# Other steps in the timetable of layer 0's mixers: a case on one core of Trainium2

## The chip, the cores and the metric

The kernel runs on one core of one Trainium2 chip. The metric is the device time of one execution in microseconds (us). Before the change three runs gave a median of 2450.46 us (2445.37 to 2455.84). The engines are named by their short names in the rows: PE is TensorE (PEld its weight loads), DVE VectorE, ACT ScalarE, POOL GpSimd and SP SyncE.

## The reference

A two-layer encoder works on 2048 tokens of 1024 channels. Layer 0 splits its projection into a head group with HGRN2 (the "a" side) and one with RWKV7 (the "b" side); layer 1 is a gated linear recurrence (RG-LRU). Each layer modulates its input by a conditioning vector and ends in a projection, a gated residual and a layer norm.

```python
cond = jax.nn.silu(c)
for l in range(DEPTH):
    mod = cond @ ada_w[l] + ada_b[l]
    shift, scale, gate = jnp.split(mod, 3, axis=-1)
    h = x * (1.0 + scale[:, None]) + shift[:, None]
    if l % 2 == 0:
        u = h @ ev_w_in[e]
        qA, fA, iA, gA, rB, kB, vB, zB, gB = jnp.split(u, EVEN_SPLITS, axis=-1)
        oA = hgrn2_chunkwise(qA, fA, iA, lbs[e], a_norm_g[e])
        oB, vf = rwkv7_mix(rB, kB, vB, zB, ...)
        mixed = jnp.concatenate([oA * silu(gA), oB * silu(gB)], axis=-1)
        y = mixed @ ev_w_out[e]
    else:
        ...
    x = layer_norm(DEEPNORM_ALPHA * x + (1.0 + gate[:, None]) * y, ln_g[l], ln_b[l])
```

HGRN2 works in chunks of 64 tokens: a decay log_f, its running sum b, products of queries and keys under exp(b_t - b_s), and a state carried from chunk to chunk. RWKV7 is a recurrence with a rank-one correction per token:

```python
sa = jnp.einsum('bhvk,bhk->bhv', S, a_t)
S = S * w_t[:, :, None, :] + sa[..., None] * b_t[:, :, None, :] + v_t[..., None] * k_t[:, :, None, :]
y_t = jnp.einsum('bhvk,bhk->bhv', S, r_t)
```

The kernel does it in chunks of 64 tokens too, which asks for the inverse of a triangular matrix per chunk. It is solved in pieces of 16 tokens, these are merged to 32, and these to 64.

## The kernel before, in words

The sequence is worked in two super-blocks (`sb`, 1024 tokens), each in two blocks (`b`, 512 tokens). For each super-block layer 0 runs a mixer stage, `mix0`, and an output projection; then layer 1 does the same. In the trace the mixers of layer 0 lie at 35 to 780 us and at 880 to 1604 us.

A float32 product of large matrices is made of three products of split operands (`mm3`, L431 to L433). One projection of 128 channels for 512 tokens (`pp_...`) is 24 matmuls.

The order of TensorE's work in `mix0` is written out by a timetable. The generator `projections()` goes in steps of six projection matmuls: 16 steps for the low-rank inputs of RWKV, 192 for the projections, and then the gates. Beside it stands a list of tasks, each a generator with the step at which it is due. After each step every due task runs to its next `yield n`, and is due again n steps later. There are four groups of heads (g0 to g3) with two blocks each (b0, b1); a block is named g1b0 and the like. For each there are three tasks: `rate_steps` (decay rates, matmuls `pw`), `b_steps` (RWKV) and `a_steps` (HGRN2). A fourth kind, `late_modulation_steps`, computes modulation columns that are wanted later: eight weight tiles are loaded and accumulated on VectorE (`acc`, L166, L168), then the columns are summed over the partitions by a matmul (`pm`, L190).

Only TensorE is put in the order of the timetable (`tc.manual_schedule(engines={nc.tensor.engine})`). The other engines' order is decided by the scheduler, which sees the program in the order in which the generators emitted it.

The steps of `b_steps`, by their products on TensorE, counted from the block's start: `pss` (L831) at 2, the chunk products `psc` (L872) at 8 and 10, a solve of 16 x 16 pieces on VectorE and GpSimd, the 32-token merge with `plq` (L961) at 22, `pzq` (L971) at 24 and `plx` (L990) at 26, the 64-token merge `pz` (L1001) at 28, then `pwv`, `pmq`, the states `pn` (one chunk per step), `py` at 42 and `pvr` at 44. Between `pzq` and `plx` lie four copies to `x_b` on ScalarE (L975) and a transpose to `xm` on VectorE (L977). Before `pss` is used, a logarithm is taken on ScalarE (L362), which loads another activation table before and the usual one after (L356, L351).

The steps of `a_steps`: a preparation with exponentials and a logarithm on ScalarE (L606 to L608), the decay (L610), its scan (L612), two more rows and an exponential (L614 to L617), then per level two halves of a decay tile `w_a` (L631, L632), its exponential (L633) and a product with the query (L634), used by the scores `sc_a` (L646); four steps after the preparation come `pv_a` and the scores of levels 5 and 0, then the others, the state `pst` (L717, L729), the output `po_a` and a norm.

Of the kernel before, what the change touches and what calls it, by code (L numbers as in the profile page):

```python
# [68 lines left out]
def tile_encoder(  # L69
# [21 lines left out]
    NSB = NT // SBT  # L91
# [57 lines left out]
    def V(name, i):  # L149
        o = VOFF[name] + i  # L150
        return vec[:, o : o + 1]
# [27 lines left out]
    def mod_cols(l, j, acc, wtile):  # L179

        for k in range(KT):
            w = wtile(j, k)
            nc.sync.dma_start(w, ada_w[l, k * P : (k + 1) * P, j * BLK : (j + 1) * BLK])
            mod_add(acc, w, k, first=k == 0)

    def mod_vec(l, j, acc):

        pm = ps.tile([P, 4], F32, name=f"pm{l}_{j}", tag="ta")
        for i in range(4):
            nc.tensor.matmul(pm[:, i : i + 1], acc[:, i * P : (i + 1) * P], ones, start=True, stop=True)  # L190
        mod_bias(l, j, pm)

    def mod_gate(l, n, acc):

        pg = ps.tile([P, BLK], F32, name=f"pg{l}_{n}", tag="ta")
        nc.tensor.matmul(pg[0:1], ones, acc, start=True, stop=True)
        gr = up.tile([P, BLK + 3], F32, name=f"gr{l}_{n}", tag="u")[0:1, 0:BLK]
        nc.sync.dma_start(gr, ada_bg[l][:, n * BLK : (n + 1) * BLK])
        nc.vector.scalar_tensor_tensor(out=gr, in0=pg[0:1], scalar=1.0, in1=gr, op0=ALU.add, op1=ALU.add)
        nc.sync.dma_start(gate_dr[l][:, n * BLK : (n + 1) * BLK], gr)  # L200
# [51 lines left out]
    for j in (1, 3):  # L252
        mod_vec(0, j, accs[j])

    def late_modulation_steps(l, js):

        wt = ("a_e", "a_lf", "a_w", "a_w")
        for i, j in enumerate(js):
            acc = tp.tile([P, BLK], F32, name=f"acc{l}_{j}", tag=("a_b", "a_kz")[i % 2])

            def wtile(j, k):
                t = wt[k % 4]
                return tp.tile([P, BLK], F32, name=f"adw{l}_{j}_{k}", tag=t, bufs=2 if t == "a_w" else 1)

            mod_cols(l, j, acc, wtile)
            yield 6
            if j < 4:
                mod_vec(l, j, acc)
            else:
                mod_gate(l, j - 4, acc)  # L270
# [78 lines left out]
    def ln_exp_after(ins):  # L349
        with tc.issue_after(ins.ins), tc.high_priority():  # L350
            nc.scalar.preload_act_table_set(LN_EXP)  # L351
# [245 lines left out]
    def a_steps(hh, sb, b, us):  # L597
# [17 lines left out]
        kf = t2k("a_e")  # L615
        nc.scalar.activation(kf, kz, AF.Exp)
        nc.vector.tensor_sub(kz, kz, bb)  # L617

        st = st_tiles[0]
        v128 = lambda t: t.rearrange("p (j two t) -> p j two t", two=2, t=64)  # L620
# [55 lines left out]
        for j in range(4):  # L676
            js = slice(j * P, (j + 1) * P)
# [37 lines left out]
        for j in range(4):  # L715
            js = slice(j * P, (j + 1) * P)
# [20 lines left out]
        for j in range(4):  # L737
            js = slice(j * P, (j + 1) * P)
# [31 lines left out]
    xd = cst.tile([P, 8, 32], F32, name="xd")  # L770
    nc.gpsimd.memset(xd, 0.0)

    def rate_steps(p, sb, b, lr, sgi_of):

        sgi = sgi_of[p, b] = tp.tile([P, 2, BLK], F32, name=f"sgi_{p}_{sb}_{b}", tag="sgi")
        w2a2_sb = tp.tile([P, P], F32, name=f"w2a2_{p}_{sb}_{b}", tag="w2a2")
        nc.sync.dma_start(w2a2_sb, w2a2[:, p * P : (p + 1) * P])
        yield 2
        ls = slice(b * BLK, (b + 1) * BLK)

        pws = [ps.tile([P, BLK], F32, name=f"pw_{p}_{sb}_{i}_{b}", tag="tb", bufs=2) for i in range(2)]
        for i in range(2):
            rows = slice(64 * i, 64 * i + 64)
            nc.tensor.matmul(pws[i], w2a2_sb[rows], lr[rows, ls], start=True, stop=True)
        for i, bias in enumerate(("w0", "a0")):
            last = nc.scalar.activation(sgi[:, i], pws[i], AF.Sigmoid, bias=V(bias, p))
        ln_exp_after(last)
# [23 lines left out]
    def b_steps(p, sb, b, us, sgi_of):  # L811
# [168 lines left out]
        for hb in range(4):  # L980
            rs_ = slice(32 * hb, 32 * hb + 32)
            o_ = 32 * (hb % 2)
            nc.gpsimd.tensor_copy(tt[rs_, :, o_ : o_ + 32], x32[rs_])
        yield 2
        plx = ps.tile([P, 8, 32], F32, name=f"plx_{nm}", tag="tb", bufs=2)
        for c in range(8):
            for hd in range(2):
# [180 lines left out]
    def low_rank(sb, hs, lr, w_first):  # L1168
        l2 = [None, None]

        def evac_shift(b, pt):
            l2[b] = up.tile([P, BLK + 3], F32, name=f"l2_{sb}_{b}", tag="u")[:, 0 : BLK + 1]
            nc.scalar.copy(l2[b][:, 1 : BLK + 1], pt)
            if "lora" not in carry:
                nc.gpsimd.memset(l2[b][:, 0:1], 0.0)
            else:
                nc.gpsimd.tensor_copy(l2[b][:, 0:1], carry["lora"])
            lc = sp_.tile([P, 1], F32, name=f"lc_{sb}_{b}", tag="lc", bufs=2)
            nc.gpsimd.tensor_copy(lc, l2[b][:, BLK : BLK + 1])
            carry["lora"] = lc  # L1180

        def evac(b, pt):
            lrb = lr[:, b * BLK : (b + 1) * BLK]
            nc.vector.tensor_sub(lrb, pt, l2[b][:, 1 : BLK + 1])
            nc.vector.tensor_add(lrb, lrb, l2[b][:, 0:BLK])
            nc.scalar.activation(lrb[0:64], lrb[0:64], AF.Tanh)

        if sb == 0:
            yield from proj_start_steps(((f"z{sb}_1", w_first[0], evac_shift), (f"z{sb}_0", w_first[1], evac)), hs)
        else:  # L1190
            yield from proj_steps(wf_dr[1], f"z{sb}_1", hs, evac_shift, w_first[0])
            yield from proj_steps(wf_dr[0], f"z{sb}_0", hs, evac)

    def mix0(sb, hs, w_first):


        lr = tp.tile([P, SBT], F32, name=f"lr{sb}", tag="lr")
        sgi_of, tail = {}, []
        ub = [[[None, None] for _ in range(3)] for _ in range(4)]
        ua = [[[None, None] for _ in range(3)] for _ in range(4)]  # L1200

        def projections():
            yield from low_rank(sb, hs, lr, w_first)
            for g in range(4):
                for i in range(3):
                    key = f"b{sb}_{i}_{g}"
                    yield from proj_steps(w_ev[16 + 4 * i + g], key, hs, evac_lerp(key, i, g, ub[g][i]))
                for i in (1, 2, 0):
                    ct = 4 * i + g
                    key = f"a{sb}_{ct}"  # L1210
                    yield from proj_steps(w_ev[ct], key, hs, evac_u(key, (0, ct), 0, ua[g][i]))
            yield from gate_steps(
                0, sb, hs, w_ev, lambda k: 12 + k if k < 4 else 28 + k, (0, 1, 2, 4, 5, 6, 3, 7), tail,
                [dict(tag="lr"), dict(tag="sgi")],
            )

        tasks = []
        if sb == 0:
            tasks.append((18, late_modulation_steps(0, (4, 5))))
        if sb == NSB - 1:  # L1220
            tasks.append((18 if NSB > 1 else 36, late_modulation_steps(1, range(6))))
        for g in range(4):
            for b in range(2):
                early = 4 if g == 3 and b else 0
                tasks.append((34 + 48 * g + 24 * b - early, rate_steps(g, sb, b, lr, sgi_of)))
                tasks.append((40 + 48 * g + 24 * b - early, (g, b, b_steps, ub)))
                tasks.append((64 + 48 * g + 24 * b, (g, b, a_steps, ua)))

        tasks = [[at, task] for at, task in tasks]
        steps = projections()  # L1230
        now = 0
        with tc.manual_schedule(engines={nc.tensor.engine}):
            while tasks or steps is not None:
                if steps is not None and next(steps, "end") == "end":
                    steps = None
                now += 1
                for entry in list(tasks):
                    if entry[0] > now:
                        continue
                    if isinstance(entry[1], tuple):  # L1240
                        g, b, make, us = entry[1]
                        entry[1] = make(g, sb, b, us[g], sgi_of) if make is b_steps else make(g, sb, b, us[g])
                    wait = next(entry[1], None)
                    if wait is None:
                        tasks.remove(entry)
                    else:
                        entry[0] = now + wait
        return tail, load_wo(0, sb, w_evo, [
            tp.tile([P, n, BLK], F32, name=f"wo0_{sb}_{i}", tag=tag, bufs=bufs)
            for i, (n, tag, bufs) in enumerate(WO0)  # L1250
        ])
# [114 lines left out]
```

## Time and profile before

| | us |
|---|---|
| median of 3 runs | 2450.46 |
| profiled execution | 2446.24 |
| its span, first to last instruction | 2444.5 |
| TensorE busy | 2208.4 |
| VectorE busy | 1454.8 |
| ScalarE busy | 1256.6 |

One execution is recorded by the hardware profiler. A row of the timeline gives the start in the span, the duration, the engine, the line of the kernel, and in brackets the idle time of the engine before the instruction with what ended it. Matmuls of one kind that follow each other are one row with their count. [...]

### The profile page before, as it was taken

To read this page: it belongs to the slowest core of one execution; us is meant where nothing else is said; L and a number is where in the kernel's file an instruction comes from. 1 tells how busy PE (TensorE), PEld (TensorE's weight loads), DVE (VectorE), ACT (ScalarE), POOL (GpSimd) and SP (SyncE) were. 2 spreads that over 40 slices of the span, in tenths; PEclk is the share of its full clock that TensorE was granted. 3 is DMA by queue.
4 is the path that set the end of the run, shared out by engine and by line. 5 is a ranking of instruction groups with operands and counts; after the bars stand their busy time and mean duration, and the time that the engine had idled before them with its cause. 6 is when DMAs were issued, how large, how long until landed. Compare 5 with 4: busy or idle time off the path is not lost. (4 is left out here: it accounts for less than half of the span.)

```text
span 2444.5 us, 45532 instructions
## 1 busy us (share of the span) xinstructions
PE 2208.4 (90%) x18400; PEld 1738.7 (71%) x18400; DVE 1454.8 (60%) x2697; ACT 1256.6 (51%) x2027; POOL 557.2 (23%) x586
## 2 busy tenths in 40 slices
PE   5989989999987998899999999989986999996998
PEld 4767767677766876677776777768765778774776
DVE  6546667566644677565666755356766156766166
ACT  4344556545566433454455556654666344666332
POOL 3311112111112222111111111122433232433231
PEclk7989999999998999999999999989998999998999
DMA  7310111111424645111111123254313544113542
GB/s 289 93 37 24 41 32 41 38 38 38 118 70 128 207 152 175 34 34 43 25 42 35 37 83 97 72 204 143 104 65 120 169 141 137 67 57 122 167 137 103
DMA packets 185938, 229.82 MB, mean 94 GB/s; under 512 B 65912, under 2 KB 99320, under 8 KB 185728
## 3 DMA queue, kind: packets, MB, share of 16 engines
q1 hardware_dynamic: 185728, 226.92, 29.1%
q8 instruction: 144, 2.36, 0.4%
q14 instruction: 66, 0.54, 0.1%
HBM read 175.46 MB, written 51.39 MB: 93 GB/s over the span
## 5 line engine op out<-in xcount | busy, mean ns | idle before, releaser
L431 PE MATMUL pp_g<-hl_h,wh_g 128*128 128x512 f32 x512 | 212.3, 415 | 40.8 <-ACT go L574 40.8
L433 PE MATMUL pp_g<-hh_h,wl_g 128*128 128x512 f32 x512 | 204.6, 400 | 2.0 <-POOL wl_g L368 2.0
L431 PE MATMUL po<-hl_wo,wh_mx 128*128 128x512 f32 x448 | 179.3, 400 | 28.9 <-DVE hl_wo L368 24.1
L432 PE MATMUL pp_g<-hh_h,wh_g 128*128 128x512 f32 x512 | 204.9, 400 | 0.0
L433 PE MATMUL po<-hh_wo,wl_mx 128*128 128x512 f32 x448 | 177.4, 396 | 0.0
L432 PE MATMUL po<-hh_wo,wh_mx 128*128 128x512 f32 x448 | 177.2, 396 | 0.0
L368 POOL TENSOR_TENSOR wl_g<-raw_g,wh_g 128x512 fp32r<-128x512 f32 x64 | 87.2, 1363 | 377.5 <-ACT wh_g L367 342.7
L431 PE MATMUL pp_b<-hl_h,wh_b 128*128 128x512 f32 x384 | 168.5, 439 | 5.0 <-ACT cr_b L805 5.0
L431 PE MATMUL pp_a<-hl_h,wh_a 128*128 128x512 f32 x384 | 168.7, 439 | 0.0
L432 PE MATMUL pp_b<-hh_h,wh_b 128*128 128x512 f32 x384 | 153.7, 400 | 0.0
L433 PE MATMUL pp_a<-hh_h,wl_a 128*128 128x512 f32 x384 | 153.5, 400 | 0.0
L432 PE MATMUL pp_a<-hh_h,wh_a 128*128 128x512 f32 x384 | 153.3, 399 | 0.0
L433 PE MATMUL pp_b<-hh_h,wl_b 128*128 128x512 f32 x384 | 153.0, 398 | 0.0
L431 PEld LDWEIGHTS pp_g<-hl_h,wh_g 128*128 128x128 f32 x512 | 99.5, 194 | 64.7 <-ACT go L574 41.7
L368 POOL TENSOR_TENSOR wl_a<-raw_a,wh_a 128x512 fp32r<-128x512 f32 x48 | 67.7, 1416 | 329.1 <-ACT wh_a L367 329.1
L568 DVE TENSOR_TENSOR go<-go,oi 128x512 f32<-128x512 f32 x64 | 46.8, 733 | 160.6 <-ACT go L564 144.9
L368 POOL TENSOR_TENSOR wl_mx<-raw_mx,wh_mx 128x512 fp32r<-128x512 f32 x64 | 80.7, 1265 | 269.1 <-ACT wh_mx L367 269.1
L368 POOL TENSOR_TENSOR wl_b<-raw_b,wh_b 128x512 fp32r<-128x512 f32 x48 | 66.5, 1391 | 271.1 <-ACT wh_b L367 270.1
L431 PEld LDWEIGHTS po<-hl_wo,wh_mx 128*128 128x128 f32 x448 | 86.0, 192 | 48.4 <-DVE hl_wo L368 24.9
L433 PEld LDWEIGHTS pp_g<-hh_h,wl_g 128*128 128x128 f32 x512 | 99.2, 194 | 25.2 <-POOL wl_g L368 3.5
L432 PEld LDWEIGHTS pp_g<-hh_h,wh_g 128*128 128x128 f32 x512 | 99.4, 194 | 19.2
L433 PE MATMUL pp_c<-hh_h,wl_c 128*128 128x512 f32 x256 | 102.2, 400 | 8.6 <-POOL wl_c L368 8.6
(355 smaller groups left out, 5707.4 us busy)
## 6 DMA issues: line engine op xcount, KB each, us to landing
adw<-in_ada_w_dram SPq DMA_DIRECT2D x96, 256.0 KB
oi<-o_dr SPq DMA_DIRECT2D x64, 256.0 KB
m_dr<-go SPq DMA_DIRECT2D x56, 256.0 KB
raw_b<-in_w_ev_dram SPq DMA_DIRECT2D x48, 256.0 KB
raw_a<-in_w_ev_dram SPq DMA_DIRECT2D x48, 256.0 KB
raw_g<-in_w_ev_dram SPq DMA_DIRECT2D x32, 256.0 KB
wo<-in_w_evo_dram SPq DMA_DIRECT2D x32, 256.0 KB
raw_mx<-m_dr SPq DMA_DIRECT2D x32, 256.0 KB
```

Of the source, the lines that this page charges most:

```text
L368: return (eng or nc.vector).tensor_tensor(out=lo, in0=src, in1=hi.bitcast(F32), op=ALU.subtract)
L431: nc.tensor.matmul(pt, ah, bl, start=first, stop=False)
L432: nc.tensor.matmul(pt, ah, bh, start=False, stop=False)
L433: nc.tensor.matmul(pt, al, bh, start=False, stop=last)
L568: nc.vector.tensor_mul(go[b], go[b], oi[b])
```

## The change

It changes numbers in the timetable and adds one `yield`:

```diff
-    def late_modulation_steps(l, js):
+    def late_modulation_steps(l, js, gap):
...
             mod_cols(l, j, acc, wtile)
-            yield 6
+            yield gap
...
         kf = t2k("a_e")
         nc.scalar.activation(kf, kz, AF.Exp)
         nc.vector.tensor_sub(kz, kz, bb)
+        yield 2
...
-    def rate_steps(p, sb, b, lr, sgi_of):
+    def rate_steps(p, sb, b, lr, sgi_of, ahead):
...
-        yield 2
+        yield ahead
...
             nc.gpsimd.tensor_copy(tt[rs_, :, o_ : o_ + 32], x32[rs_])
-        yield 2
+        yield 4
         plx = ps.tile([P, 8, 32], F32, name=f"plx_{nm}", tag="tb", bufs=2)
...
         if sb == 0:
-            tasks.append((18, late_modulation_steps(0, (4, 5))))
+            tasks.append((10, late_modulation_steps(0, (4, 5), 14)))
         if sb == NSB - 1:
-            tasks.append((18 if NSB > 1 else 36, late_modulation_steps(1, range(6))))
+            tasks.append((4 if NSB > 1 else 38, late_modulation_steps(1, range(6), 9 if NSB > 1 else 4)))
         for g in range(4):
             for b in range(2):
-                early = 4 if g == 3 and b else 0
-                tasks.append((34 + 48 * g + 24 * b - early, rate_steps(g, sb, b, lr, sgi_of)))
-                tasks.append((40 + 48 * g + 24 * b - early, (g, b, b_steps, ub)))
-                tasks.append((64 + 48 * g + 24 * b, (g, b, a_steps, ua)))
+                at = 48 * g + 24 * b - (2 if g == 3 and b else 0)
+                tasks.append((34 + at if g or b else 2, rate_steps(g, sb, b, lr, sgi_of, 2 if g or b else 32)))
+                tasks.append((40 + at if g or b else 42, (g, b, b_steps, ub)))
+                tasks.append((62 + 48 * g + 24 * b, (g, b, a_steps, ua)))
```

In steps: in every RWKV block `plx` and all that follows it come two steps later. The HGRN2 task starts two steps earlier, and the added `yield 2` lets its decays and all its TensorE work stand at the step where they stood. The first RWKV block starts two steps later (42) with its rates at step 34, not 36, and the small weight of these rates loaded from step 2. The last block g3b1 and its rates start two steps later (206 and 200 in place of 204 and 198). The late modulation of layer 0's gates starts at step 10 with a column group every 14 steps (before: 18 and 6), that of layer 1 at step 4 every 9 (before: 18 and 6).

The first place is TensorE in g1b0. Names end in the block and a running number; the block of `plx` here is the one before the block of `pss`. Before:

```order
L433 MATMUL pp_b_0_2_0_3182<-hh_h_0_0_3_375,wl_b_0_2_0_3173 128x512
L990 MATMUL plx_b_0_0_3195<-xm_b_0_0_3139,zb_b_0_0_2398 32x32 x16
L831 MATMUL pss_b_0_1_3215<-ep_b_0_1_3167,bones 128x512
L431 MATMUL pp_b_0_2_0_3182<-hl_h_0_0_4_392,wh_b_0_2_1_3178 128x512
...
L433 MATMUL pp_b_0_2_0_3182<-hh_h_0_0_7_379,wl_b_0_2_1_3179 128x512
L1001 MATMUL pz_b_0_0_3260<-x_b_0_0_2911,lx_b_0_0_3212 32x32 x16
L668 MATMUL pv_a_0_0_3280<-ident,u_a_9_0_2698 128x128 x4
L646 MATMUL sc_a_0_0_3285<-w_a_0_0_3158,a_e_a_0_0_3155 64x32 x8
L646 MATMUL sc_a_0_0_3285<-w_a_0_0_3161 32x32 x8
```

After, the same stretch and the `pz` that follows:

```order
L433 MATMUL pp_b_0_2_0_3182<-hh_h_0_0_3_375,wl_b_0_2_0_3173 128x512
L832 MATMUL pss_b_0_1_3195<-ep_b_0_1_3167,bones 128x512
L431 MATMUL pp_b_0_2_0_3182<-hl_h_0_0_4_392,wh_b_0_2_1_3178 128x512
...
L433 MATMUL pp_b_0_2_0_3182<-hh_h_0_0_7_379,wl_b_0_2_1_3179 128x512
L991 MATMUL plx_b_0_0_3240<-xm_b_0_0_3152,zb_b_0_0_2378 32x32 x16
L669 MATMUL pv_a_0_0_3260<-ident,u_a_9_0_2673 128x128 x4
L647 MATMUL sc_a_0_0_3265<-w_a_0_0_3158,a_e_a_0_0_3098 64x32 x8
L647 MATMUL sc_a_0_0_3265<-w_a_0_0_3161 32x32 x8
...
L1002 MATMUL pz_b_0_0_3311<-x_b_0_0_2905,lx_b_0_0_3257 32x32 x16
```

`plx` has gone behind `pss` of the next block and another twelve projection matmuls, and stands straight ahead of `pv_a` and the scores; `pz`, which stood there, follows twelve projection matmuls later.

The second place is VectorE at the same block. Before, the tile `xm` (L977) stands behind the first rows of the HGRN2 decays:

```order
L610 SCALAR_TENSOR_TENSOR a_lf_a_0_0_3149<-u_a_5_0_2411,a_e_a_0_0_3145 128x512
L612 SCALAR_TENSOR_TENSOR a_b_a_0_0_3151<-smask,a_lf_a_0_0_3149 128x512
L632 TENSOR_TENSOR w_a_0_0_3161<-a_b_a_0_0_3151 128x8x32
L634 TENSOR_TENSOR w_a_0_0_3158<-w_a_0_0_3158,u_a_1_0_2999 128x256
L614 TENSOR_TENSOR a_kz_a_0_0_3153<-a_lf_a_0_0_3149,u_a_5_0_2411 128x512
L977 STREAM_TRANSPOSE xm_b_0_0_3139<-x_b_0_0_2911 128x256
L617 TENSOR_TENSOR a_kz_a_0_0_3153<-a_kz_a_0_0_3153,a_b_a_0_0_3151 128x512
L631 TENSOR_TENSOR w_a_0_0_3161<-a_kz_a_0_0_3153,a_b_a_0_0_3151 128x8x32
L833 TENSOR_SCALAR b_m_b_0_1_3217<-pss_b_0_1_3215 128x512
L634 TENSOR_TENSOR w_a_0_0_3161<-w_a_0_0_3161,u_a_1_0_2999 128x8x32
```

After (all lines past 617 are one higher):

```order
L610 SCALAR_TENSOR_TENSOR a_lf_a_0_0_3092<-u_a_5_0_2391,a_e_a_0_0_3088 128x512
L612 SCALAR_TENSOR_TENSOR a_b_a_0_0_3094<-smask,a_lf_a_0_0_3092 128x512
L978 STREAM_TRANSPOSE xm_b_0_0_3152<-x_b_0_0_2905 128x256
L633 TENSOR_TENSOR w_a_0_0_3161<-a_b_a_0_0_3094 128x8x32
L614 TENSOR_TENSOR a_kz_a_0_0_3096<-a_lf_a_0_0_3092,u_a_5_0_2391 128x512
L635 TENSOR_TENSOR w_a_0_0_3158<-w_a_0_0_3158,u_a_1_0_2965 128x256
L617 TENSOR_TENSOR a_kz_a_0_0_3096<-a_kz_a_0_0_3096,a_b_a_0_0_3094 128x512
L834 TENSOR_SCALAR b_m_b_0_1_3197<-pss_b_0_1_3195 128x512
L632 TENSOR_TENSOR w_a_0_0_3161<-a_kz_a_0_0_3096,a_b_a_0_0_3094 128x8x32
...
L632 TENSOR_TENSOR w_a_0_0_3288<-a_kz_a_0_0_3096,a_b_a_0_0_3094 128x16x16
L633 TENSOR_TENSOR w_a_0_0_3288<-a_b_a_0_0_3094 128x16x16
L635 TENSOR_TENSOR w_a_0_0_3161<-w_a_0_0_3161,u_a_1_0_2965 128x8x32
```

`xm` stands right behind the scan; the product L635 that finishes the decay tile `w_a_0_0_3161` now stands behind `b_m`, `zr` and two rows of the next level's tile.

The third is ScalarE there. Before, from the table load and the preparation's first step, then from the copies of `x_b`:

```order
L351 ACT_TABLE_LOAD
L606 ACTIVATE a_e_a_0_0_3145<-u_a_5_0_2411 128x512
...
L975 COPY x_b_0_0_2911<-pzq_b_0_0_3102 16x8x16 x4
L616 ACTIVATE a_e_a_0_0_3155<-a_kz_a_0_0_3153 128x512
L994 COPY lx_b_0_0_3212<-plx_b_0_0_3195 32x256 x2
L633 ACTIVATE w_a_0_0_3161<-w_a_0_0_3161 128x512
L840 ACTIVATE ep_b_0_1_3167<-sgi_0_1_2984 128x8x64
L356 ACT_TABLE_LOAD
L362 ACTIVATE b_m_b_0_1_3217<-b_m_b_0_1_3217 128x512
L351 ACT_TABLE_LOAD
L835 ACTIVATE b_m_b_0_1_3217<-b_m_b_0_1_3217,kk_bias 128x512
```

After:

```order
L351 ACT_TABLE_LOAD
L606 ACTIVATE a_e_a_0_0_3088<-u_a_5_0_2391 128x512
...
L976 COPY x_b_0_0_2905<-pzq_b_0_0_3115 16x8x16 x4
L629 ACTIVATE w_a_0_0_3158<-a_lf_a_0_0_3092 128x512
L616 ACTIVATE a_e_a_0_0_3098<-a_kz_a_0_0_3096 128x512
L841 ACTIVATE ep_b_0_1_3167<-sgi_0_1_2947 128x8x64
L356 ACT_TABLE_LOAD
L362 ACTIVATE b_m_b_0_1_3197<-b_m_b_0_1_3197 128x512
L351 ACT_TABLE_LOAD
L634 ACTIVATE w_a_0_0_3161<-w_a_0_0_3161 128x512
L836 ACTIVATE b_m_b_0_1_3197<-b_m_b_0_1_3197,kk_bias 128x512
```

The exponential of the decay tile `w_a_0_0_3161` (L633, now L634) stood ahead of `ep_b` and the logarithm with its two table loads, and now stands behind them. L606 stands behind its table load in both.

At the opening of the second super-block the first columns `pm` of layer 1 followed two full products `pp_b`; they now stand inside the second low-rank product (`pp_z`), 18 matmuls ahead of the first `pp_b`.

## Rows read from the trace of the kernel before

**Rows 1.** The page: busy time, share, instructions of each engine.

```profile
PE 2208.4 (90%) x18400; PEld 1738.7 (71%) x18400; DVE 1454.8 (60%) x2697; ACT 1256.6 (51%) x2027; POOL 557.2 (23%) x586
```

**Rows 2.** Waits of TensorE, whole span: in total, times, longest.

```profile
PE plx_b L990 <- DVE xm_b L977: 29.9, 14, 3.9
...
PE psc_b L872 <- DVE bk_b L859: 12.8, 2, 8.4
PE sc_a L646 <- DVE w_a L634: 11.8, 8, 3.2
...
PE psc_b L872 <- DVE zb_b L879: 7.4, 12, 0.8
```

**Rows 3.** Timeline of TensorE in g1b0: start, duration, instruction, [idle before].

```profile
323.14 0.39 PE L433 MATMUL pp_b<-hh_h,wl_b 128*128 128x512 f32 x1
327.42 1.07 PE L990 MATMUL plx_b<-xm_b,zb_b 32*32 32x32 f32 x32 [3.90 <-DVE xm_b L977]
...
335.80 0.66 PE L646 MATMUL sc_a<-w_a,a_e_a 128*64 128x32 f32 x16
```

**Rows 4.** Timeline of VectorE in g1b0.

```profile
312.41 0.45 DVE L951 STREAM_TRANSPOSE xn_b<-xd 128x256 f32<-128x256 f32 x1 [4.94 <-DMA xd<-xd_b]
...
323.09 2.12 DVE L612 TENSOR_TENSOR_SCAN a_b_a<-smask,a_lf_a 128x512 f32<-128x512 bf16 x1
...
326.94 0.43 DVE L977 STREAM_TRANSPOSE xm_b<-x_b 128x256 f32<-128x256 f32 x1
...
331.14 0.41 DVE L634 TENSOR_TENSOR w_a<-w_a,u_a 128x256 f32<-128x256 f32 x1
```

**Rows 5.** Timeline of ScalarE in g1b0.

```profile
323.56 1.08 ACT L975 COPY x_b<-pzq_b 16x128 f32<-16x128 f32 x4
327.11 0.63 ACT L616 ACTIVATE a_e_a<-a_kz_a 128x512 f32<-128x512 f32 x1 [2.47 <-DVE a_kz_a L614]
...
331.25 1.28 ACT L356 ACT_TABLE_LOAD   x1
332.54 0.63 ACT L362 ACTIVATE b_m_b<-b_m_b 128x512 f32<-128x512 f32 x1
```

**Rows 6.** Timeline of TensorE in the next block, g1b1.

```profile
401.14 0.69 PE L990 MATMUL plx_b<-xm_b,zb_b 32*32 32x32 f32 x32 [1.59 <-DVE xm_b L977]
401.76 1.12 PE L831 MATMUL pss_b<-ep_b,bones 128*128 128x512 f32 x2
...
405.54 0.69 PE L1001 MATMUL pz_b<-x_b,lx_b 32*32 32x32 f32 x32
406.17 0.66 PE L668 MATMUL pv_a<-ident,u_a 128*128 128x128 f32 x4
```

**Rows 7.** Timeline of VectorE in g1b1.

```profile
400.65 0.43 DVE L977 STREAM_TRANSPOSE xm_b<-x_b 128x256 f32<-128x256 f32 x1
```

**Rows 8.** Windows: length, busy (count) per engine, granted clock, DMA share, GB/s; then a sum.

```profile
326.60:333.40 6.80, 5.98 (x42) 4.21 (x43) 3.51 (x7) 4.74 (x8) 1.17 (x3) 0.50 0.01 2
...
616.70:620.10 3.40, 3.40 (x9) 2.64 (x8) 3.37 (x5) 1.56 (x4) 1.63 (x1) 0.50 0.41 103
...
sum 27.20, PE 26.36 PEld 18.45 DVE 17.33 ACT 19.43 POOL 5.77; mean PE 4.39 PEld 3.07 DVE 2.89 ACT 3.24 POOL 0.96
...
401.10:407.80 6.70, 6.66 (x115) 5.11 (x115) 4.34 (x9) 5.93 (x9) 1.13 (x3) 1.00 0.01 2
625.00:630.00 5.00, 3.99 (x37) 3.34 (x38) 3.09 (x8) 3.37 (x8) 0.00 (x0) 0.70 0.40 109
```

**Rows 9.** Timeline of TensorE in g3b0.

```profile
615.75 0.69 PE L990 MATMUL plx_b<-xm_b,zb_b 32*32 32x32 f32 x32 [1.92 <-DVE xm_b L977]
...
626.01 0.45 PE L646 MATMUL sc_a<-w_a 128*32 128x32 f32 x16 [3.22 <-DVE w_a L634]
```

**Rows 10.** Timelines in the second super-block's opening: VectorE (first row), TensorE.

```profile
905.74 2.33 DVE L168 SCALAR_TENSOR_TENSOR acc<-adw,cond,acc 128x512 f32<-128x512 f32 x3
...
907.98 0.39 PE L431 MATMUL pp_b<-hl_h,wh_b 128*128 128x512 f32 x1
...
966.85 1.44 PE L872 MATMUL psc_b<-zr_b,bk_b 64*128 64x128 f32 x10 [8.44 <-DVE bk_b L859]
```

## Prediction

> **What bounds the kernel now.** I read the page's first parts, then TensorE's waits, then three stretches of the timeline, then the granted clock in windows. TensorE is busy for 90% of the span, no other engine for more than 60% [rows 1]; what this change can win is TensorE's idle time in the mixer stages, and the slower clock that follows some of it. Of the list of waits [rows 2] four bear on the change: the merge product `plx` on the transposed tile `xm` (29.9 us, 14 times, once per RWKV block but the first), `psc` on `bk` (two first blocks, 12.8), the HGRN2 scores `sc_a` on a decay tile `w_a` (11.8, 8 times) and `psc` on `zb` (7.4, twelve small ones). Only the first has its own wait edited in all blocks; the steps between `psc` and `plq` of a first block stay what they were.
>
> The place to see is the third block of the first super-block, g1b0 [rows 3 to 5]. TensorE ends its projections at 323.5 and stands 3.90 us before `plx` at 327.42 [rows 3]. On VectorE, `xm` starts at 326.94, behind the scan L612 (end 325.21) and three instructions of the HGRN2 block, L632, L634 and L614 [rows 4], though the copies of its input `x_b` were done at 324.64 (323.56 + 1.08) [rows 5]. The next block, g1b1, has the same with 1.59 us: projections to 399.55, `plx` at 401.14 [rows 6]. [...]
>
> **The change part by part.** *The merge.* In after, `pss` of the next block and two steps of projections stand ahead of `plx`. Their price is read from g1b1, where nothing is waited for: from `pss` at 401.76 to `pz` at 405.54, 3.78 us [rows 6]. So in g1b0 TensorE would come to `plx` at about 323.5 + 3.78 = 327.3, and VectorE's order has `xm` right behind the scan, done at about 325.7. Cover is 1.6 us. In g1b1 TensorE comes at 399.55 + 3.78 = 403.3, against `xm` done at 401.08 (400.65 + 0.43) [rows 7], with L614 now ahead of it: about 401.7. All 14 gaps go: −29.9 us, and with them the 13.6 us of the slow clock.
>
> *What is late next.* `plx` was a gate that held TensorE back for the HGRN2 block too. Behind it comes `sc_a`, which in g1b0 began at 335.80, with its `w_a` (L634) done at 331.55 [rows 3, 4]. In after TensorE is there at about 327.3 + 0.62 (`plx`, until the next began) + 0.66 (`pv_a`) = 328.6 [rows 6] and ends the first of the two score groups at 329.1. The preparation is meant to be two steps earlier, but its first instruction L606 still stands on ScalarE behind the table load that follows the next rates, so it starts no earlier. And ScalarE's order puts the exponential of `w_a` (L634 of after) behind a table load, the logarithm L362 and a second load like the first: 1.28 + 0.63 + 1.28 us [rows 5]. VectorE puts two rows of the next level ahead of the product that `sc_a` reads. Walked through at the durations of the rows: the scan ends at 325.2, `xm`, L633 and L614 at 326.8, L616 at 327.5, `ep_b` 328.1, load 329.4, logarithm 330.0, load 331.3, exponential 332.0, product 332.4. The second group of `sc_a` would wait 3.3 us. The chain of such a block starts late because the last state of the HGRN2 block before it (L729) stands behind `xn`, which waits for a transfer until 312.41 [rows 4]; the new order shortens that by some tenths, and I take 2.9 us for g1b0 and g2b0 (even blocks). For g1b1 the same walk has L614 done at 401.3, L616 at 402.0, `ep_b` 402.6, load 403.9, logarithm 404.5, load 405.8, exponential 406.4 and the product at 406.9, with TensorE there at 405.1: 1.8 us, taken for g0b1, g1b1 and g2b1 (odd blocks). For the two blocks of the last head pair, where the longest waits are 1.92 at `plx` and 3.22 at `sc_a` [rows 9], I take 2.5 together, since no block follows that puts its logarithm in between. Sum per super-block 3 × 1.8 + 2 × 2.9 + 2.5 = 13.7, both 27.4; the two waits of 3.22 are replaced by it, −6.4: **+21.0 us**.
>
> Bounds of this term: the walk is 1.3 us too late if one table load (1.28) runs while nothing waits for it, which leaves 0.5 and 1.6 a block and some 10 us in all, less 6.4: +4. It is too early if the group-norm steps L1082 and L1083, which now stand among the preparation's ScalarE instructions, push it; at the 0.63 us of such an instruction one of the two makes 2.4 in odd blocks, both make about 4.0 in even ones, and 2.5 stays: 35.4 − 6.4 = +29.
>
> *The clock behind the new waits.* 1.59 us never cost the clock, 1.92 us did in both super-blocks, 3.9 us did each time [rows 8, 9]. [...] The six waits of 1.8 us lie between the two cases; 1.2 us for all. **+8.0 us**, bounds 0 and 24 (14 × 1.7).
>
> [...]
>
> *`psc` on `zb`.* The second pair of `psc` has `pmq` ahead of it in after, twice as many matmuls as `pn`, which stood there. Of the 7.4 us [rows 2] I take 3 as gone; bounds 0 and 7.4. `py` and `pvr` move two steps with the rest and nobody waits for them. But the copy `lq` now stands behind two group-norm steps on ScalarE: `pzq` could wait 0 to 0.4 us in the even blocks, taken as nothing.
>
> *Late modulation.* In the second super-block the columns `pm` move from behind the second product `pp_b`, where TensorE waited for nothing, into the low-rank products, 18 matmuls ahead of the first `pp_b` at 907.98; the 12 matmuls of a step pair start 0.23 us apart, so that is 903.9. The accumulator is ready at 908.07 (905.74 + 2.33) [rows 10], paced by the transfers of its weights. That is a new wait of 4.2 us with a slow stretch of 1.7 behind it. All that TensorE loses here is in front of the 8.44 us wait of `psc` at 966.85 for `bk` [rows 10], whose VectorE work ends when it ends. Of the 5.9 us I take 2 as staying (VectorE's products of `u_b` now stand behind more accumulations, which can push `bk` as well): **+2 us**, bounds −2 and +8. In the first super-block the two gate columns go to places with nothing behind them: 0, and the first rates two steps earlier likewise, since the first `psc` waits for `bk` and not for the rates' products; each ±1.
>
> *Sum.* The profiled execution took 2446.24 us (span 2444.5), 4.2 less than the median of 2450.46. −29.9 − 13.6 + 21.0 + 8.0 − 3.0 + 2.0 = −15.5, so 2430.7 by the profiled execution and 2435 by the median. I give **2432 us**.
>
> **The rivals.** *All of it is gained.* The chain to `w_a` is quick enough, or the scheduler's order hides it: −29.9 − 13.6 − 3 + 4 + 2 = −40.5: 2406 us. For it: the eight waits on `w_a` in before are 0.9 us in the mean but for the two of 3.22. Against: the table loads that now stand ahead of the exponential.
>
> *The wait only changes its name.* The HGRN2 preparation is bound by its own chain through ScalarE, and TensorE stands at `sc_a` as long as it stood at `plx`; the clock falls as often: 2446 us. For it: L606 isn't earlier on ScalarE, although the timetable says so. Against: `xm` no longer stands behind 1.7 us of VectorE work (325.2 to 326.94), and ScalarE sat idle 2.47 us ahead of L616 [rows 5].
>
> *Slower.* At `sc_a`, with the waits at their upper bound, 2.4 us in the odd blocks and 4.0 in the even ones, each of the 14 is long enough for the clock, where before only six were: −29.9 − 13.6 + 29 + 24 + 2 = +11.5: 2458 us. It decides from the point where the odd blocks' wait passes 1.9 us, 0.1 more than I work out, which is why it has a chance at all.
>
> **How the numbers follow.** Part given back 0.44 (2432; its own range 2420 to 2442), all gained 0.20, name only 0.22, slower 0.14. Of the first, 0.36 lie more than 0.5% (12 us, about what a measurement of this kernel can tell from no change) below the median of before. Faster 0.36 + 0.20 = 0.56; same 0.08 + 0.20 = 0.28; slower 0.14 + 0.02 = 0.16. The range leaves out half of the two outer cases: 2404 to 2456.
>
> **What would show it.** In the waits of the changed kernel: `plx` on `xm` gone or under 3 us; `sc_a` on `w_a` up from 11.8 to some 30, longest in the even blocks; `pm` on an accumulator with about 4 us early in the second super-block, and `psc` on `bk` shorter there. In windows behind the even blocks' `sc_a`, the clock at 0.50 once. Wrong if `plx` still waits, if `sc_a` doesn't, or if another product (`pzq` on `lq`, `pwv` on `tt`) takes over.

## The result and the profile after

The changed kernel takes 2516.24 us (median of 4 runs, 2513.08 to 2519.16) against 2447.91 for the kernel before; the ratio is 1.0274, 95% interval 1.0243 to 1.0305. It is slower by 68 us, and the forecast was 16 us faster with a range that ended at 2456. The profiled execution has a span of 2517.4 us, 72.9 more than before.

The page's first part, which answers to [rows 1]:

```profile
PE 2246.1 (89%) x18400; PEld 1770.3 (70%) x18400; DVE 1452.8 (58%) x2697; ACT 1255.1 (50%) x2025; POOL 560.5 (22%) x586
```

TensorE executes the same 18400 matmuls and is busy 37.7 us longer (2208.4 to 2246.1), at a mean granted clock of 0.932 where it was 0.952. The rest of the longer span, 35.2 us, is idle time of TensorE (236.1 to 271.3).

The granted clock (PEclk) stands in the windows as a share, 1.00 where it is highest. What 0.50 means for the matmuls is seen in the kernel before: projection matmuls of 128x512 start 0.43 us apart in g1b0, in the window at 0.50, and 0.23 us apart in g1b1, in the window at 1.00 [rows 8] (TensorE's timeline, two of each):

```profile
331.57 0.63 PE L431 MATMUL pp_b<-hl_h,wh_b 128*128 128x512 f32 x1
332.00 0.63 PE L432 MATMUL pp_b<-hh_h,wh_b 128*128 128x512 f32 x1
...
403.41 0.39 PE L431 MATMUL pp_a<-hl_h,wh_a 128*128 128x512 f32 x1
403.64 0.39 PE L432 MATMUL pp_a<-hh_h,wh_a 128*128 128x512 f32 x1
```

Where it is idle stands in the list of waits of the changed kernel (in total, times, longest), which answers to [rows 2]:

```profile
PE pn_b L1055 <- DVE sb_b L1058: 44.0, 19, 3.6
...
PE sc_a L647 <- DVE w_a L635: 34.2, 15, 3.7
...
PE psc_b L873 <- DVE bk_b L860: 14.8, 4, 4.8
...
PE pz_b L1002 <- ACT lx_b L995: 6.5, 2, 3.3
...
PE plx_b L991 <- DVE xm_b L978: 1.8, 2, 0.9
PE psc_b L873 <- DVE zb_b L880: 1.3, 2, 0.8
```

The waits of `plx` on `xm` have gone, 29.9 to 1.8 us, and those of `psc` on `zb`, 7.4 to 1.3. `sc_a` on `w_a` is up by 22.4. And at the head of the list stands a wait that the prediction does not have at all: `pn`, the states of the RWKV block, on `sb`, the copy that VectorE scales out of `pn`. It had 1.9 us in before, in the last block of each super-block, where no solve follows.

One place, on TensorE: the states of g1b0, which run beside the solve of the next block, g1b1 (timeline; start, duration, [idle before]):

```profile
366.17 0.33 PE L1055 MATMUL pn_b<-sb_b,zb_b 64*64 64x64 f32 x4
...
370.50 0.33 PE L1055 MATMUL pn_b<-sb_b,zb_b 64*64 64x64 f32 x4
...
375.08 0.48 PE L1055 MATMUL pn_b<-sb_b,zb_b 64*64 64x64 f32 x4 [2.65 <-DVE sb_b L1058]
```

A state is a chain of eight: TensorE adds one chunk to `pn`, VectorE scales the sum into `sb`, and the next chunk's product reads `sb`. The product of 370.50 ends at 370.8 and the next has to wait until 375.08. VectorE's timeline of the same stretch (L1058 is the copy of a state, L941 a row of the solve):

```profile
364.70 0.28 DVE L1058 TENSOR_SCALAR sb_b<-pn_b,lam_b 128x64 f32<-128x64 f32 x1 [2.25 <-PE pn_b L1055]
367.88 1.26 DVE L941 TENSOR_TENSOR pr_b<-xt_b,ai_b 128x2 f32<-128x2 f32 x1 [2.90 <-POOL ai_b L933]
...
369.25 0.28 DVE L1058 TENSOR_SCALAR sb_b<-pn_b,lam_b 128x64 f32<-128x64 f32 x1
...
369.91 1.54 DVE L662 COPY_PREDICATED st<-lmask,sc_a 64x128 f32<-64x128 uint8 x4
371.46 0.43 DVE L703 TENSOR_TENSOR a_kz_a<-a_kz_a,a_b_a 128x256 f32<-128x256 f32 x1
371.81 0.42 DVE L704 TENSOR_TENSOR u_a<-u_a,a_b_a 128x256 f32<-128x256 f32 x1
...
373.19 1.06 DVE L941 TENSOR_TENSOR pr_b<-xt_b,ai_b 128x28 f32<-128x28 f32 x1
...
374.50 0.21 DVE L941 TENSOR_TENSOR pr_b<-xt_b,ai_b 128x32 f32<-128x32 f32 x1
374.74 0.28 DVE L1058 TENSOR_SCALAR sb_b<-pn_b,lam_b 128x64 f32<-128x64 f32 x1
```

The `sb` that follows the product of 366.17 starts at 369.25, behind a first row of the solve (L941) that itself had waited 2.90 us for GpSimd's `ai`. The one after it, wanted at 370.8, starts at 374.74: ahead of it in VectorE's queue are the solve's next rows, four predicated copies of scores (L662) and two rows of the HGRN2 block. VectorE's timeline in before, for the same states and the same solve, shows it idle and waiting for TensorE's next product:

```profile
356.66 0.28 DVE L1057 TENSOR_SCALAR sb_b<-pn_b,lam_b 128x64 f32<-128x64 f32 x1
...
359.85 0.28 DVE L1057 TENSOR_SCALAR sb_b<-pn_b,lam_b 128x64 f32<-128x64 f32 x1 [0.78 <-PE pn_b L1054]
361.71 0.28 DVE L1057 TENSOR_SCALAR sb_b<-pn_b,lam_b 128x64 f32<-128x64 f32 x1 [1.58 <-PE pn_b L1054]
...
365.71 0.28 DVE L1057 TENSOR_SCALAR sb_b<-pn_b,lam_b 128x64 f32<-128x64 f32 x1 [2.21 <-PE pn_b L1054]
367.56 0.28 DVE L1057 TENSOR_SCALAR sb_b<-pn_b,lam_b 128x64 f32<-128x64 f32 x1 [1.56 <-PE pn_b L1054]
...
370.84 0.15 DVE L940 TENSOR_TENSOR pr_b<-xt_b,ai_b 128x2 f32<-128x2 f32 x1
```

Five states are out before the solve's first row at 370.84. The order in which VectorE executed the two shows it without any time. S is one of the eight states of g1b0 and r one of the fifteen product rows of g1b1's solve:

```
before   SSSSSrrrrSrrrrSrrrrrrSr
after    SSrSrrrrrrSrrrSrrrrrSSS
```

The order alone doesn't set the price: before, the states of g3b0 stood among the rows of a solve as well (rrSrrrrrrSrrrSrrrrSSSSS in the first super-block), and `pn` waited for none of them. One thing that differs is that the row ahead of a state now waits itself. The first row of each solve needs `ai` from GpSimd; before, VectorE stood still for it only in the first block of each super-block, and in the changed kernel in all sixteen blocks (VectorE's waits, before and after):

```profile
DVE pr_b L940 <- POOL ai_b L932: 9.4, 2, 7.8
...
DVE pr_b L941 <- POOL ai_b L933: 74.8, 16, 8.7
```

A state's copy behind such a row waits with it, as the one at 369.25 above, behind a wait of 2.90 us.

The clock, in windows of the changed kernel (length, busy per engine, granted clock, DMA share, GB/s):

```profile
299.60:303.00 3.40, 3.40 (x67) 3.08 (x65) 3.06 (x13) 1.17 (x2) 0.00 (x0) 0.50 0.00 0
374.60:381.40 6.80, 6.32 (x76) 5.46 (x77) 5.64 (x22) 1.82 (x4) 0.00 (x0) 0.50 0.13 41
412.20:419.00 6.80, 5.47 (x28) 4.32 (x28) 5.66 (x11) 5.58 (x12) 0.00 (x0) 0.50 0.00 0
```

The first lies behind a wait of `pn` of 3.51 us, the second begins within the wait of 2.65 us shown above, the third within a wait of `sc_a` of 3.11. All ran at a granted clock of 0.50.

At g1b0 the second group of `sc_a` waits 2.54 us, near what the prediction took, and for the reason given, the exponential behind two table loads (ScalarE's timeline):

```profile
331.49 1.28 ACT L356 ACT_TABLE_LOAD   x1 [0.82 <-DVE b_m_b L834]
332.79 0.63 ACT L362 ACTIVATE b_m_b<-b_m_b 128x512 f32<-128x512 f32 x1
333.44 1.28 ACT L351 ACT_TABLE_LOAD   x1
334.73 0.63 ACT L634 ACTIVATE w_a<-w_a 128x512 f32<-128x512 f32 x1
```

and on TensorE:

```profile
332.68 0.66 PE L647 MATMUL sc_a<-w_a,a_e_a 128*64 128x32 f32 x16
335.88 0.45 PE L647 MATMUL sc_a<-w_a 128*32 128x32 f32 x16 [2.54 <-DVE w_a L635]
```

### The profile page after: what moved, and what is told of

Its sections match the earlier page's. It is cut to its first block, busy times and chain, and to the rows that moved or that the text cites. A ratio compares the mean times of both kernels' runs of the same rounds, so it can differ in the third digit from the quotient of the medians.

```text
span 2517.4 us, 45573 instructions
## 1 busy us (share of the span) xinstructions
PE 2246.1 (89%) x18400; PEld 1770.3 (70%) x18400; DVE 1452.8 (58%) x2697; ACT 1255.1 (50%) x2025; POOL 560.5 (22%) x586
## 3 DMA queue, kind: packets, MB, share of 16 engines
q1 hardware_dynamic: 185728, 226.92, 28.1%
## 5 line engine op out<-in xcount | busy, mean ns | idle before, releaser
L431 PE MATMUL po<-hl_wo,wh_mx 128*128 128x512 f32 x448 | 179.1, 400 | 29.8 <-DVE hl_wo L368 24.3
L941 DVE TENSOR_TENSOR pr_b<-xt_b,ai_b 128x2 f32<-128x2 f32 (+14 forms) x240 | 84.9, 354 | 81.7 <-POOL ai_b L933 74.8
```

Source lines behind the costliest of these rows:

```text
L431: nc.tensor.matmul(pt, ah, bl, start=first, stop=False)
L941: nc.vector.tensor_mul(pv_, xt[:, 0:n, 0 : i + 1], av)
```

## The experiments

Each version was timed beside the kernel before on the same chip; ratios are to that kernel, with a 95% interval.

**The four parts alone, each put into the kernel before.** The merge: the diff is the one line of the change ahead of `plx`.

```diff
-        yield 2
+        yield 4
         plx = ps.tile([P, 8, 32], F32, name=f"plx_{nm}", tag="tb", bufs=2)
```

> Before with one edit: the two steps more ahead of plx (and so of all later steps of a block), nothing else of the change. Theory A (the states): the state products pn now fall into the solve of the next block, their evacuation on VectorE queues behind rows of the solve, and this alone makes the loss. Then pn waits for sb some 35 to 45 us in all, the clock drops behind them, and the time is 2490 to 2515 us against 2448. Rival B (the HGRN2 preparation's new place and the scores): the merge alone only takes away the 29.9 us before plx; pn waits under 10 us, 2415 to 2445 us. Rival C (late modulation and first block make the loss): about 2448 or less.

Measured: 2504.84 us against 2448.54, 1.0233 (1.0208 to 1.0258). This one edit alone costs 56 us; the whole change costs 68. Its waits:

```profile
PE sc_a L646 <- DVE w_a L634: 46.8, 18, 3.3
PE pn_b L1054 <- DVE sb_b L1057: 35.1, 14, 3.6
...
PE pz_b L1001 <- ACT lx_b L994: 11.6, 4, 3.3
```

The HGRN2 task's earlier start:

```diff
         nc.vector.tensor_sub(kz, kz, bb)
+        yield 2
...
-                tasks.append((64 + 48 * g + 24 * b, (g, b, a_steps, ua)))
+                tasks.append((62 + 48 * g + 24 * b, (g, b, a_steps, ua)))
```

> Before with one edit: the HGRN2 task starts two steps earlier, with the yield of 2 steps behind its preparation. Theory A: no new wait of pn; the orders of VectorE and ScalarE near xm change little, 2440 to 2455 us. Rival B: the exponential of w_a queues behind the table loads, sc_a waits for w_a over 25 us instead of 11.8 and the time is over 2465 us.

Measured: 2463.33 us, 1.006 (1.004 to 1.008): 15 us slower, more than theory A expected, and not by rival B's way, since `sc_a` waits 11.0 us there. `plx` waits 35.6 in place of 29.9 and TensorE is busy 8.9 us longer. VectorE's order has one row more ahead of `xm` in g1b1, L614, and the wait there is 2.31 us where it was 1.59. The mean granted clock of the profiled execution is 0.948 where it was 0.952.

The late modulation's numbers:

```diff
...
-            tasks.append((18, late_modulation_steps(0, (4, 5))))
+            tasks.append((10, late_modulation_steps(0, (4, 5), 14)))
...
-            tasks.append((18 if NSB > 1 else 36, late_modulation_steps(1, range(6))))
+            tasks.append((4 if NSB > 1 else 38, late_modulation_steps(1, range(6), 9 if NSB > 1 else 4)))
```

> Before with one edit: the late modulation's starts and gaps (10 and 14 in the first super-block, 4 and 9 in the second). Theory A: pm waits about 5 us early in the second super-block and psc on bk there falls from 8.4 to about 5, so 2444 to 2454 us. Rival C: the DMA-paced accumulations push the evacuations behind them, over 2465 us.

Measured: 2452.64 us, 1.0011 (0.9996 to 1.0027): no difference that these runs can tell. In the second super-block `pm` waits 7.2 us, and `psc` on `bk` 6.0.

The first and last block's shifts and the rates:

```diff
...
-                early = 4 if g == 3 and b else 0
-                tasks.append((34 + 48 * g + 24 * b - early, rate_steps(g, sb, b, lr, sgi_of)))
-                tasks.append((40 + 48 * g + 24 * b - early, (g, b, b_steps, ub)))
+                at = 48 * g + 24 * b - (2 if g == 3 and b else 0)
+                tasks.append((34 + at if g or b else 2, rate_steps(g, sb, b, lr, sgi_of, 2 if g or b else 32)))
+                tasks.append((40 + at if g or b else 42, (g, b, b_steps, ub)))
```

> Before with one edit: the first RWKV block two steps later and its rates two steps earlier, the last block and its rates two steps later. Theory A: 2440 to 2456 us, since the relation of the states to the next block's solve stays as it was but for the first and the last pair (pn waits up to 6 us). Rival C: over 2465 us.

Measured: 2443.53 us, 0.9976 (0.9961 to 0.9991): 5 us faster. But `pn` waits 12.5 us for `sb`, in the first and the last pair, twice what theory A allowed. The four sum to 56.3 + 14.8 + 4.1 − 5.0 = 70, against 68 for the whole change.

**The change without the merge.** In the changed kernel:

```diff
-        yield 4
+        yield 2
         plx = ps.tile([P, 8, 32], F32, name=f"plx_{nm}", tag="tb", bufs=2)
```

> After with one edit: the 32-token merge back at its old steps, all else of the change kept. Theory A (the merge's shift makes the loss through the states): pn waits fall from 46 to under 13 us, plx waits come back to about 26 to 36 us, and the time is 2455 to 2468 us, the sum of the other three parts taken alone (2448 + 15 + 4 - 5). Rival B (the parts only hurt together): below 2450 us.

Measured: 2464.66 us, 1.0057 (1.0029 to 1.0085), as theory A has it; `pn` waits 10.2 us on `sb` and `plx` 29.8.

**The states out of VectorE's queue.**

```diff
-            nc.vector.tensor_scalar_mul(states[c + 1], pn[:, c], lam[:, c : c + 1])
+            nc.scalar.activation(states[c + 1], pn[:, c], AF.Identity, scale=lam[:, c : c + 1])
```

> After with one edit: each state is scaled and copied out by ScalarE, not by VectorE, at the same steps. Theory A (the evacuation queues behind rows of the next block's solve on VectorE): pn waits fall from 46 us to under 12, the slow stretches behind them go, and the time is 2445 to 2470 us, with sc_a's 34 us of waits left. Rival D (the states are late for another reason, as their inputs or the product itself): pn still waits, then for ScalarE, over 30 us, and the time stays at 2500 to 2520 us. Rival E (the copies on ScalarE delay the chain to w_a): pn free, but sc_a waits over 50 us, 2480 to 2510 us.

Measured: 2479.08 us, 1.0106 (1.0085 to 1.0128), so 37 us back by moving the copy alone. `pn` waits 4.9 us, `sc_a` the same 34.2 as in the changed kernel. The time is 9 us above theory A's; `pk_a` and `pzq`, which hardly waited in the changed kernel, now wait 21 us:

```profile
PE sc_a L647 <- DVE w_a L635: 34.2, 18, 3.7
...
PE pk_a L711 <- DVE a_kz_a L703: 12.1, 8, 2.3
...
PE pzq_b L972 <- ACT lq_b L966: 9.0, 6, 1.7
...
PE pn_b L1055 <- ACT sb_b L1058: 4.9, 6, 1.6
```

**The states at their old steps, on VectorE.**

```diff
-        yield 2
+        yield 1
         for c4 in range(2):
             cs4 = slice(4 * c4, 4 * c4 + 4)
             pw = ps.tile([P, 4, 2, 64], F32, name=f"pwv_{nm}_{c4}", tag=("yb", "cg")[c4])
...
-        yield 2
+        yield 1
         for c4 in range(2):
             cs4 = slice(4 * c4, 4 * c4 + 4)
             pm = ps.tile([P, 4, 2, 64], F32, name=f"pmq_{nm}_{c4}", tag=("yb", "cg")[c4])
```

> After with one edit: the two yields ahead of pwv and pmq are 1 and not 2, so that the states, py and pvr stand at the steps of before, two ahead of those of after, while plx stays late. Theory A: pn waits fall from 46 us to under 15; new waits of pwv or pmq on their copies, 10 to 30 us, take the place of a part; 2470 to 2505 us. Rival D: pn waits as long as in after, 2505 us or more.

Measured: 2463.64 us, 1.0049 (1.0033 to 1.0065): two steps less take back 53 of the 68 us, more than theory A expected. `pn` waits 11.5 us on `sb`, and VectorE's order has five states ahead of the solve again in the middle blocks, as before; the first row of the solve waits for `ai` in six blocks, not sixteen. `sc_a` fell too, to 13.7, and `pz` rose from 6.5 to 18.8, so the 53 us are not the states' alone.

**The second term, the scores.** The merge alone, with one more edit in the HGRN2 task:

```diff
         w_5, w_0 = decays(5), decays(0)
-        yield 4
+        yield 6
```

> The merge edit alone (two steps more ahead of plx, in before) with one more: 6 steps, not 4, between the HGRN2 preparation and its first scores. The merge alone took 2505 us, with 35 us of waits of pn and 47 of sc_a. Theory A (two separate terms): sc_a waits under 12 us, pn 30 to 50, and the time is 2460 to 2485 us. Rival F (when the scores no longer wait, the states wait so much longer): pn over 60 us, 2495 us or more.

Measured: 2485.92 us, 1.0153 (1.012 to 1.0186), 19 less than the merge alone and just above the expected span. `sc_a` waits 1.2 us in place of 46.8, `pn` 30.7 in place of 35.1; `pz` on `lx`, whose copies stand behind the same table loads, waits 27.5 in place of 11.6. (18.8 of it stand in the list as "issue", a wait with no cause in the profile; in the first version of parts, below, whose list has the same, `pz` of g1b0 starts at 332.23, 0.1 us after the first copy of `lx` ends, 331.76 + 0.36.) In the changed kernel itself this edit makes a deadlock, with the states where they are there and with the states put back, so neither has a time.

With the states on ScalarE as well (the diff shown above):

> The merge edit alone with both: the scores two steps later, and the states copied out by ScalarE. Theory A: neither pn nor sc_a waits over 12 us, pz on lx some 25 us as in the version made of parts, and the time is 2430 to 2450 us, 55 to 75 less than the merge alone. Rival F: 2470 us or more.

Measured: 2461.64 us, 1.0046 (1.003 to 1.0062). The edits are worth 19 and then 24 us, so two terms; but the merge is still no gain when both are gone, and the expectation was missed by 12 us: `pz` waits 33 us.

**Versions made of parts.** The first is the last one above with the first and last block's shifts:

> A version made of parts: before, with the first and last block's shifts, the late merge, the states copied out by ScalarE, and the first scores of the HGRN2 task two steps later (6, not 4, behind its preparation). Theory A: neither plx nor pn waits, sc_a waits under 15 us, and the time is 2400 to 2425 us. Rival E: the chain through ScalarE to w_a is what bounds, sc_a or pz waits 30 us and more, 2440 us or above.

Measured: 2434.08 us, 0.9928 (0.9905 to 0.9951), above what was expected. Two waits are left of those that the change bears on, `pz` with 28.8 us and `psc` on `bk`, which is longer than before (21.0 against 12.8):

```profile
PE psc_b L872 <- DVE bk_b L859: 21.0, 6, 5.9
PE pz_b L1001 <- issue: 20.4, 10, 3.4
...
PE pz_b L1001 <- ACT lx_b L994: 8.4, 8, 2.0
...
PE pn_b L1054 <- ACT sb_b L1057: 5.9, 4, 3.0
...
PE sc_a L646 <- DVE w_a L634: 2.4, 2, 1.2
```

With the copies `lx` on VectorE:

```diff
-            nc.scalar.copy(lx[r1], plx[r1])
+            nc.vector.tensor_copy(lx[r1], plx[r1])
```

> The version made of parts, with the two copies lx on VectorE in place of ScalarE. If the copies of lx behind the table loads on ScalarE are the last wait of that version (pz waits 28.8 us there), pz falls under 12 us and the time to 2410 to 2428 us. If VectorE's own queue is as late (the scan and the decays), pz waits 20 us or more and the time stays at 2430 to 2440 us.

Measured: 2438.52 us, 0.9972 (0.9962 to 0.9983). `pz` falls to 1.9 us as expected, those under "issue" included, and the time does not fall: `sc_a` on `w_a` is back at 34.9.

And the shifts with the states on ScalarE, but neither the late merge nor the later scores:

> Before with the first and last block's shifts and the states copied out by ScalarE, the merge and the HGRN2 task at their old steps. If the late merge brings something once the states are out of its way, this is slower than the version made of parts: plx waits 26 to 30 us and the time is 2438 to 2450 us. If not, 2425 to 2435 us.

Measured: 2433.5 us, 0.9948 (0.9931 to 0.9965), with `plx` waiting 31.2 us. It is as fast as the first version of parts, which has the late merge and the later scores on top (the intervals overlap), so these two bring nothing together that the runs can tell. All three versions lie below both kernels, below the kernel before by 0.3 to 0.7%.

## Why the prediction was wrong

*The step that failed* is in the part on `psc` and `zb`: "`py` and `pvr` move two steps with the rest and nobody waits for them". Between `pmq` and `py` lie the eight states, and the sentence left them out. They are the one part of a block that goes to VectorE and back every step, and two steps later they meet the next block's solve in VectorE's queue. Measured: 44.0 us of waits with 1.9 before, shown to be that queue by the states on ScalarE (4.9 us, 37 us of time) and by the states two steps back (11.5 us; 53 us of time, in which `sc_a`'s fall is contained). In the middle blocks VectorE's order has five states ahead of the solve before and two after; the prediction read the orders of both programs at `plx`, `xm` and `w_a` only.

*The clock* was the second miss, and by size the equal of the first. I had −13.6 and +8.0 in the sum, and the matmuls took 37.7 us more. No run shows the 13.6 us, nor the 1.7 us that the +8.0 and the late modulation's +2 take for a slow stretch: both were estimates, half of the 27.2 us at 0.50 [rows 8] and half of 3.4. What the rows show is the spacing of the projection matmuls, 0.43 us at 0.50 and 0.23 at 1.00, by which I estimate 12.7 of the 27.2 us; and what the changed kernel shows is the 37.7. The forecast counted four new waits long enough for the clock; of `pn` and `sc_a` together there were 22 of 1.9 us and more.

*What held.* The waits of `plx` went (28.1 of 29.9 us). `sc_a` came up by 22.4 us, forecast 21.0, for the reason worked out: 2.5 us in g1b0 and g2b0, where I had 2.9, and 3.1 in g1b1 and g2b1, where I had 1.8. That the sums agree is in part luck: g0b1, for which I had 1.8, waited for nothing, and g0b0, for which I had nothing, waited 3.71 in the second super-block; with the merge alone `sc_a` rose by 35.0. `psc` on `zb` lost 6.1 where I took 3. In the second super-block `pm` waited 5.0 us (forecast 4.2) and `psc` on `bk` fell from 8.44 to 4.82 there; the late modulation alone came out at +4 (interval −1 to +7), forecast +2. The slower rival named `sc_a` and the clock, and its mechanism was a part of what came; its price lacked the states. One bound was added up wrongly: the lower bound of `sc_a`'s term leaves out the 2.5 us of the last pairs, which the upper bound keeps; with them it is +8, not +4, and the best rival's time 2410, not 2406.

*What wasn't counted* either: the HGRN2 task's earlier start costs 15 us by itself, through `plx` and the clock. The prediction gave it no price because it starts no earlier; what it changes is VectorE's order. In the whole change `plx` is out of the way, and how much of the 15 us is in its 68 is open: the four parts add up to 70, which allows all of it.

*What stays open.* With the first and last block's shifts, worth 5 us alone, the merge with both edits (2461.64 us) becomes the first version of parts (2434.08), 28 us in a comparison that lies across two sets of runs. Most of it can be placed. The version without the shifts has three waits in the last pair of both super-blocks, between 620 and 662 and between 1453 and 1497 us, that the version with them hasn't:

```profile
PE pzt_b L922 <- ACT bkt_b L912: 11.6, 2, 6.1
...
PE psc_b L872 <- ACT lx_b L994: 8.3, 2, 4.2
...
PE plx_b L990 <- DVE xm_b L977: 4.2, 2, 2.1
```

So it is the last block's shift that a late merge asks for, as far as the waits tell; the shift of that block by itself was not run.

## What to carry to other kernels

When a step is moved in a timetable, list every product behind it that goes to another engine and back, and read in that engine's queue what it now stands behind, and whether that is itself still waiting; a chain with one round trip per step is the first to look at. A wait that is hidden by another wait comes back when that one goes: here `plx` stood behind the scan, `sc_a` and `pz` behind the table loads, and each fix moved the stop by one. Price the clock with the waits: here the matmuls took 37.7 us more beside 35.2 us more of idle time.

## What the runs showed of the hardware

With waits that came every 38 us or so in the middle blocks, each of 2.2 to 3.6 us, TensorE's mean granted clock was 0.932 where it had been 0.952, and the same matmuls took 37.7 us more while the idle time grew by 35.2: a microsecond of waiting cost about two. The merge alone has the same price (27.6 us of idle time, 27.0 of busy time, at a mean clock of 0.935); with the scores two steps later it was 24.0 and 12.3, at 0.942, so it is no constant. And the length of a wait does not settle the clock. Before, the wait of 1.59 us in g1b1 was followed by a stretch at 1.00 [rows 6, 8]; in the changed kernel one of 1.24 us, in g3b0, was followed by a stretch at 0.50. TensorE's timeline there:

```profile
644.24 0.62 PE L647 MATMUL sc_a<-w_a 128*32 128x32 f32 x16 [1.24 <-DVE w_a L635]
```

and the windows behind it and ahead of it:

```profile
644.30:647.70 3.40, 3.40 (x23) 2.76 (x24) 3.34 (x8) 3.29 (x7) 0.00 (x0) 0.50 0.23 89
640.50:644.20 3.70, 2.51 (x56) 1.79 (x54) 1.34 (x4) 3.66 (x5) 0.00 (x0) 1.00 0.38 92
```

The stretch ahead had TensorE busy for 2.51 of 3.70 us, and the idle 1.19 are that one wait. In the second super-block the same wait, of the same length, was followed by a stretch at 1.00 (timeline, then window):

```profile
1514.88 0.45 PE L647 MATMUL sc_a<-w_a 128*32 128x32 f32 x16 [1.24 <-DVE w_a L635]
...
1514.90:1518.30 3.40, 3.40 (x34) 2.59 (x36) 3.34 (x8) 3.28 (x7) 0.00 (x0) 1.00 0.20 63
```

What made the difference, these rows don't show.
